# Feature-major layer norms of a hybrid encoder layer: pairwise sums, a running sum, and one more product run ahead

## The chip, the cores and the metric

The kernel runs on one core of a Trainium2 chip. The metric is the device time of one execution in microseconds (us); of several runs the median is given. The matmul engine is called PE, VectorE is DVE, ScalarE is ACT, GpSimd is POOL and SyncE, which issues the DMAs, is SP.

## The reference

One encoder layer is computed for 1024 prompt frames and 64 frames of a running stream, 1088 tokens of 1024 features, all in fp32:

```python
z = x @ w_in                                  # 1024 -> 8200 columns
y_a = silu(layer_norm(dw, ln_a_g, ln_a_b)) @ w_a_out      # dw: causal depthwise conv of a GLU
y_b = (sigmoid(z_o) * hn) @ w_b_out                       # hn: normed mLSTM output
merged = sigmoid(g_a) * y_a + sigmoid(g_b) * y_b
x1 = layer_norm(ALPHA * x + merged @ w_out, ln1_g, ln1_b)
ff = square(relu(x1 @ w_ff1)) @ w_ff2
x2 = layer_norm(ALPHA * x1 + ff, ln2_g, ln2_b)
```

A `layer_norm` takes mean and variance over the 1024 features of a token. The outputs are `x2` and the convolution's and mLSTM's last states. The change touches the first two of the three layer norms, `ln_a` and `ln1`.

## The kernel before, in words

**Layout.** From the input projection to the last feed-forward block, activations are held feature-major: a tile `[128, 8, 384]` has feature `k*128+p` at partition `p`, slot `k`, and tokens along the columns. The 1088 tokens are cut into three chunks of 384, 384 and 320 (`CHUNKS`). Every product is made in about fp32 precision from three matmuls of a rounded high part and a low part (`mm3`, L327 to L332: high by high, high by low, low by high), so each operand is first split: ACT copies the high part, DVE subtracts for the low part (`split`, L334 to L342). One output tile of 128 features by one chunk is a *product* (`product`, L312): 8 slots by 3 matmuls, 24 matmuls into one bank of PSUM.

**The norm over partitions.** Since features lie along partitions and slots, `ln_feature` (L670) sums in two steps: over the eight slots on DVE (`total`, L677: a `tensor_reduce` of four slots, twice), and over partitions with a small matmul of that sum by a matrix of 1/1024 (L690, L691, high and low part). Then each half of four slots is centred by DVE in place (L699) and squared by ACT into a tile `sq` (L701), both squares are reduced (L702, L703), added (L704) and split (L705), and six tiny matmuls give the variance token by token (L711, L714). DVE adds epsilon (L716), POOL raises to the power -0.5 (L717), DVE spreads the result on a diagonal (L719), it is split, and two matmuls by ones give it to all partitions (L725, L726). Last, the eight slots are multiplied by it in four pairs (L729) and `finish` scales and shifts on ACT; in `ln1` it also splits each finished pair into `x1h`, `x1l`, the operand of the feed-forward part (L815 to L818). The split after a sum is called through the helper, so it is recorded at L336 (ACT) and L339 (DVE), on the tiles `sh` and `sl`.

**What sets the order.** A norm is a generator that gives way at each `yield`. It sits in a queue (`BG["misc"]`) and is stepped once by `slot()` (L119), which is called after each product is issued; `waits` gives the number of further slots between its parts. So a norm's small matmuls stand in PE's queue behind a set number of products; the first matmul of each part is pinned there (`pin`). The order of all else on each engine's queue is made by a planner when the program is compiled, from what it takes to be ready, and may differ from the order of the text. Each engine works through its own queue in order.

**The stages around the change.** `ln_a` (L740) norms the convolution's output, read back from DRAM chunk by chunk, while `w_b_out` products run. `out_proj` (L830) makes `merged @ w_out` chunk by chunk: for each of eight feature tiles `j` it loads a tile `sx` of x (from the pool `st` of five buffers), makes the product, evicts it with `ALPHA*x` added into `Y2` (L845), and calls `slot()`. When a chunk is done its `ln1` is queued, so it runs beside the next chunk's products. The last chunk's norm is started by hand at `j == 4` (L847) for its first reduction, and goes on beside the first feed-forward products: `first_units` (L995) makes the first two `w_ff1` pieces' products for chunks 0 and 1 only, then the third piece's product for chunk 0 (L1003), and then the two held products of chunk 2, whose operand the last norm has just made. `unit` (L319) takes the product that was run ahead when it comes to that piece. `post_r` (L880) squares the relu and splits sums and differences of it (`hvh`, `hvl`) for the block products of `w_ff2` that follow.

Of the kernel before, what the change touches and what calls it, by code (L numbers as in the profile page):

```python
# [9 lines left out]
F32 = mybir.dt.float32  # L10
F32R = mybir.dt.float32r
AF = mybir.ActivationFunctionType
ALU = mybir.AluOpType
AX = mybir.AxisListType
# [7 lines left out]
P = 128  # L22
KT = D // P
# [7 lines left out]
CN = 384  # L31
# [13 lines left out]
def bcast(ap, shape):  # L45
    return ap.to_broadcast(shape)
# [3 lines left out]
def hybrid_layer(ctx, tc, x_prompt, x_sample, cache_conv, state_C, state_n, state_m, w_in, b_gate,  # L50
# [4 lines left out]
    V, S, G, TE = nc.vector, nc.scalar, nc.gpsimd, nc.tensor  # L55
    w_in = w_in[0]

    def pool(name, bufs=1, stack=ctx, **kw):
        kw.setdefault("reuse_waits", "tile")
        if kw.get("space") is DRAM:  # L60
# [12 lines left out]
    pools = {"whl": pool("whl", 2, stack=whs, side="right"), "psg": pool("psg", 3, stack=pre, space=PSUM),  # L73
             "psm": pool("psm", 5, stack=pre, space=PSUM)}
    stp = pool("st", 5, stack=pre)
# [11 lines left out]
    def gtile():  # L87
        return pools["psg"].tile([P, 512], F32, tag="m", name="g")
# [13 lines left out]
    BG = {"mlstm": deque(), "conv": deque(), "misc": deque()}  # L102
# [12 lines left out]
    def drain(kind):  # L115
        while step(kind):
            pass

    def slot():  # L119
        busy = step("mlstm")  # L120
        CREDIT["conv"] = min(CREDIT["conv"] + (1.0 if busy else 1.7), 4.0)
        while CREDIT["conv"] >= 1.0 and step("conv"):
            CREDIT["conv"] -= 1.0
        step("misc")
# [182 lines left out]
            V.tensor_copy(cols[:n, b:b + nb], ps[:n, 0:nb].rearrange("p c (h z) -> p c h z", z=32)[:, :, :, 0:4])  # L307


    early, later = [], []  # L310

    def product(hi, lo, ci):  # L312
        n = CHUNKS[ci][1]
        ps = gtile()
        for k in range(KT):
            mm3(ps[:, :n], hi[:, k, :], lo[:, k, :], XO["h"][ci][:, k, :n], XO["l"][ci][:, k, :n], k == 0, k == KT - 1)
        return ps

    def unit(hi, lo, post, chunks=(0, 1, 2)):  # L319
        for ci in chunks:  # L320
            ps = early.pop() if early and ci == 0 else product(hi, lo, ci)
            while later:
                later.pop()()
            post(ci, *CHUNKS[ci], ps)
            slot()
# [8 lines left out]
    def split(hi, lo, src, scale=None, pinned=False):  # L334
        if scale is None:
            a = S.activation(hi, src, AF.Copy)  # L336
            if pinned:
                pin(a)
            V.tensor_tensor(lo, src, hi.bitcast(F32), ALU.subtract)  # L339
        else:  # L340
            S.activation(hi, src, AF.Copy, scale=scale)
            V.scalar_tensor_tensor(lo, src, scale, hi.bitcast(F32), ALU.mult, ALU.subtract)  # L342
# [324 lines left out]
            MB.append(fp.tile([P, KT, CN], F32, tag="f", name="mb"))  # L667
        BG["misc"].append(ln_a())

    def ln_feature(y, n, sc, square, finish, waits):  # L670
        def across(p, k=4):
            return bcast(p[:, None, :n], [P, k, n])

        def tiles():
            return (sc.tile([P, CN], d, tag=t, name=t) for t, d in (("s", F32), ("sh", F32R), ("sl", F32R)))

        def total(out, t, m=CN):  # L677
            V.tensor_reduce(out[:, :n], t[:, :, :n].rearrange("p k t -> p t k"), AX.X, ALU.add)  # L678

        s2 = stp.tile([P, CN], F32, tag="st", name="s2")  # L680
        total(s2, y[:, 0:4])
        yield
        s, sh, sl = tiles()
        total(s, y[:, 4:8])
        V.tensor_tensor(s[:, :n], s[:, :n], s2[:, :n], ALU.add)
        split(sh[:, :n], sl[:, :n], s[:, :n])
        for _ in range(waits[0]):
            yield
        pm = mtile()
        pin(TE.matmul(pm[:, :n], mean1, sh[:, :n], start=True, stop=False))  # L690
        TE.matmul(pm[:, :n], mean1, sl[:, :n], start=False, stop=True)  # L691
        s, sh, sl = tiles()
        s2 = sc.tile([P, CN], F32, tag="s2", name="s2")
        if n < CN:
            G.memset(s[:, n:], 0.0)
        sq = []
        for kh in range(2):
            yh = y[:, 4 * kh:4 * kh + 4, :n]
            V.tensor_tensor(yh, yh, across(pm), ALU.subtract)  # L699
            sq.append(square())  # L700
            S.activation(sq[kh][:, :, :n], yh, AF.Square)  # L701
        total(s, sq[0])  # L702
        total(s2, sq[1])  # L703
        V.tensor_tensor(s[:, :n], s[:, :n], s2[:, :n], ALU.add)  # L704
        split(sh, sl, s)  # L705
        for _ in range(waits[1]):
            yield
        pv = mtile()
        for t in range(3):
            ts = slice(t * P, (t + 1) * P)  # L710
            a = TE.matmul(pv[:, 2 * t:2 * t + 2], sh[:, ts], mean1[:, 0:2], start=True, stop=False)  # L711
            if t == 0:
                pin(a)
            TE.matmul(pv[:, 2 * t:2 * t + 2], sl[:, ts], mean1[:, 0:2], start=False, stop=True)  # L714
        st = small.tile([P, 20], F32, tag="ln", name="ln")
        V.tensor_scalar(st[:, 0:3], pv[:, 0:6:2], EPS, None, ALU.add)  # L716
        G.tensor_tensor(st[:, 3:6], st[:, 0:3], bcast(mhalf, [P, 3]), ALU.pow)  # L717
        s, sh, sl = tiles()
        V.tensor_tensor(s.rearrange("p (t q) -> p t q", q=P), bcast(ident[:, None, :], [P, 3, P]),  # L719
                        bcast(st[:, 3:6, None], [P, 3, P]), ALU.mult)  # L720
        split(sh, sl, s)
        for _ in range(waits[2]):
            yield
        pr = mtile()
        pin(TE.matmul(pr[:, :n], ones, sh[:, :n], start=True, stop=False))  # L725
        TE.matmul(pr[:, :n], ones, sl[:, :n], start=False, stop=True)  # L726
        for k0 in range(0, KT, 2):
            yh = y[:, k0:k0 + 2, :n]
            V.tensor_tensor(yh, yh, across(pr, 2), ALU.mult)  # L729
            for k in range(k0, k0 + 2):  # L730
                finish(k, y[:, k, :n])
        yield
# [73 lines left out]


    X1H, X1L, Y2 = [], [], []
    last_ln = []

    def ln1(ci):
        n = CHUNKS[ci][1]

        def finish(k, z):
            S.activation(z, z, AF.Identity, scale=vecs[:, k, R_G1:R_G1 + 1], bias=vecs[:, k, R_B1:R_B1 + 1])  # L815
            if k % 2:
                ks = slice(k - 1, k + 1)
                split(X1H[ci][:, ks, :n], X1L[ci][:, ks, :n], Y2[ci][:, ks, :n])  # L818
        X1H.append(ph.tile([P, KT, CN], F32R, tag="p", name="x1h"))
        X1L.append(pl.tile([P, KT, CN], F32R, tag="p", name="x1l"))  # L820

        def square():
            return pools["lnq" if ci == 2 else "ln1"].tile([P, 4, CN], F32, tag="sq", name="sq")
        yield from ln_feature(Y2[ci], n, pools["ln1"], square, finish, ((1, 3, 2), (1, 3, 1), (1, 2, 1))[ci])
        if ci == 2:
            lnq.close()
            lns.close()
            pools["hw0"] = pool("hw0", 1, stack=win)

    def out_proj():  # L830
        drain("misc")
        enter(1)
        set_operand(MB)
        MH, ML = XO["h"], XO["l"]
        for ci, (o, n) in enumerate(CHUNKS):
            Y2.append(fp.tile([P, KT, CN], F32, tag="f", name="y2"))
            for j in range(KT):
                s = stp.tile([P, CN], F32, tag="st", name="sx")
                nc.sync.dma_start(s[:, :n], xTD[j * P:(j + 1) * P, o:o + n])
                js = slice(j % 4 * P, j % 4 * P + P)  # L840
                ps = gtile()
                for k in range(KT):
                    mm3(ps[:, :n], WOH[j // 4][:, k, js], WOL[j // 4][:, k, js], MH[ci][:, k, :n], ML[ci][:, k, :n],
                        k == 0, k == KT - 1)
                V.scalar_tensor_tensor(Y2[ci][:, j, :n], s[:, :n], ALPHA, ps[:, :n], ALU.mult, ALU.add)  # L845
                slot()
                if ci == 2 and j == 4:  # L847
                    last_ln.append(ln1(ci))
                    next(last_ln[0])
            if ci < 2:  # L850
                BG["misc"].append(ln1(ci))
        drain("misc")
        BG["misc"].append(last_ln[0])
        step("misc")

    N(out_proj)


# [136 lines left out]
    def first_units(kh, hi, lo):  # L995
        post = post_r(0, kh, True)
        unit(hi, lo, post, (0, 1))
        held.append((hi, lo, post))
        if kh == 1:
            pools["whl"] = pools["whl2"]  # L1000
            third = 2 + next(i for i, p in enumerate(pieces) if p[3] == 1)
            wsplit(third)
            early.append(product(*his[third], 0))  # L1003
            drain("misc")
            for h in held:
                unit(*h, (2,))
            whs.close()
            pools["hw1"] = pool("hw1", 1, stack=win)
# [103 lines left out]
    raws, his = {}, {}  # L1112
# [69 lines left out]
```

## Time and profile before

| | us |
|---|---|
| median of 3 runs (1985.12, 1987.09, 1988.74) | 1987.09 |
| the profiled execution, its own time | 1988.86 |
| the profiled execution, span from first to last instruction | 1986.8 |
| PE busy in the span | 1938.1 |
| DVE busy in the span | 1425.0 |
| ACT busy in the span | 642.8 |

The span is what the trace covers; the profiled execution's own time is 2.1 us longer. Mean granted clock of PE was 0.991 of full speed. Rows of groups read: line, engine, operation, tile written and tiles read, shapes, count, then busy us, mean ns of one, and idle time of the engine before them with what ended it.

### The profile page before, as it was taken

The page shows a single profiled execution, that of the slowest core. Times are in us where ns is not written, and L with a number is a line of the kernel's source. Part 1 is how long each engine was busy: PE and PEld are TensorE (multiplying, and loading weights), DVE is VectorE, ACT ScalarE, POOL GpSimd, SP SyncE. Part 2 cuts the span into 40 slices and gives each one's busy share as a digit, 9 for nine tenths or more (in the row PEclk, how much of TensorE's full clock was granted, in tenths as well). Part 3 has the DMA queues.
Part 4 walks back from the last instruction along what each step waited for, and adds up shares of the span by engine and source line. Part 5 has one row for each costly group of instructions (what it writes and reads, how often), then busy time and mean ns, then how long its engine had stood idle before and what let it go on. Part 6 is the DMA issues. An engine that isn't in the chain of part 4 may idle for free.

```text
span 1986.8 us, 30495 instructions
## 1 busy us (share of the span) xinstructions
PE 1938.1 (98%) x12396; PEld 1914.4 (96%) x12396; DVE 1425.0 (72%) x2717; ACT 642.8 (32%) x1206; POOL 124.9 (6%) x232
## 2 busy tenths in 40 slices
PE   8999999999999999999999998999999999999996
PEld 7999999999999999999999998999999999999995
DVE  3856876787678767878874559867685858677547
ACT  4323322332233223323352214523233232414242
POOL 1112210001000100000000000000000000000005
PEclk9999999999999999999999999999999999999998
DMA  4122312121112211226235210111211111111212
GB/s 140 44 79 58 119 48 57 52 74 52 55 34 66 70 55 43 60 93 205 84 102 158 76 42 14 43 54 33 59 38 54 53 44 54 33 54 43 75 43 80
DMA packets 171744, 131.06 MB, mean 66 GB/s; under 512 B 8271, under 2 KB 166463, under 8 KB 171603
## 3 DMA queue, kind: packets, MB, share of 16 engines
q1 hardware_dynamic: 171603, 129.11, 21.7%
q8 instruction: 97, 1.59, 0.3%
q14 instruction: 44, 0.36, 0.1%
HBM read 104.39 MB, written 24.63 MB: 65 GB/s over the span
## 4 chain that ended last, share of the span: by engine, by line
PE 83%; DVE 9%; issue 3%; ACT 1%; POOL 1%; DMA 1%; SPq 0%; POOLq 0%; ACTq 0%; DVEq 0%
PE g L328 26%; PE g L331 26%; PE g L332 26%; DVE s L678 2%; PE m L328 1%; PE m L332 1%; PE m L331 1%; DVE o L1101 1%; DVE acc L567 1%; DVE ln L650 0%; DVE a L699 0%; DVE y L699 0%; PE m L461 0%; DMA x<-in_x_prompt_dram 0%; PE m L1061 0%
## 5 line engine op out<-in xcount | busy, mean ns | idle before, releaser
L328 PE MATMUL g<-xh,wh 128*128 128x384 f32 (+1 forms) x1920 | 637.7, 332 | 0.0
L331 PE MATMUL g<-xl,wh 128*128 128x384 f32 (+1 forms) x1920 | 632.0, 329 | 0.0
L332 PE MATMUL g<-xh,wl 128*128 128x384 f32 (+1 forms) x1920 | 631.5, 329 | 0.0
L328 PEld LDWEIGHTS g<-xh,wh 128*128 128x128 f32 x1920 | 363.7, 189 | 0.4 <-ACT xh L336 0.2
L331 PEld LDWEIGHTS g<-xl,wh 128*128 128x128 f32 x1920 | 363.5, 189 | 0.3
L332 PEld LDWEIGHTS g<-xh,wl 128*128 128x128 f32 x1920 | 363.1, 189 | 0.1
L567 DVE SCALAR_TENSOR_TENSOR acc<-glu,vecs,acc 128x1118 f32<-128x1118 f32 x240 | 331.6, 1382 | 3.5
L336 ACT ACTIVATE wh<-wr 128x1024 fp32r<-128x1024 f32 (+1 forms) x168 | 166.0, 988 | 445.9 <-PE g L331 355.7
L339 DVE TENSOR_TENSOR wl<-wr,wh 128x1024 fp32r<-128x1024 f32 (+1 forms) x168 | 190.7, 1135 | 113.8 <-ACT wh L336 110.9
L328 PE MATMUL g<-x1h,wh 128*128 128x384 f32 (+1 forms) x768 | 253.4, 331 | 0.0
L331 PE MATMUL g<-x1l,wh 128*128 128x384 f32 (+1 forms) x768 | 253.1, 330 | 0.0
L332 PE MATMUL g<-x1h,wl 128*128 128x384 f32 (+1 forms) x768 | 252.8, 329 | 0.0
L331 PE MATMUL g<-hvl,wh 128*128 128x272 f32 x784 | 223.7, 288 | 0.0
L332 PE MATMUL g<-hvh,wl 128*128 128x272 f32 x784 | 221.9, 288 | 0.0
L328 PE MATMUL g<-hvh,wh 128*128 128x272 f32 x784 | 221.4, 290 | 0.0
L977 DVE TENSOR_TENSOR y<-g,y 128x272 f32<-128x272 f32 (+1 forms) x540 | 157.2, 340 | 26.9 <-PE g L332 25.1
L328 PEld LDWEIGHTS g<-hvh,wh 128*128 128x128 f32 x784 | 146.0, 189 | 1.7 <-DVE y L977 1.3
L331 PEld LDWEIGHTS g<-hvl,wh 128*128 128x128 f32 x784 | 147.5, 188 | 0.0
L332 PEld LDWEIGHTS g<-hvh,wl 128*128 128x128 f32 x784 | 146.5, 188 | 0.0
L331 PEld LDWEIGHTS g<-x1l,wh 128*128 128x128 f32 x768 | 144.9, 189 | 0.1
L332 PEld LDWEIGHTS g<-x1h,wl 128*128 128x128 f32 x768 | 144.9, 189 | 0.0
L328 PEld LDWEIGHTS g<-x1h,wh 128*128 128x128 f32 x768 | 144.6, 188 | 0.1
(272 smaller groups left out, 2423.6 us busy)
## 6 DMA issues: line engine op xcount, KB each, us to landing
wr<-in_w_in_dram SPq DMA_DIRECT2D x64, 512.0 KB
wr<-in_w_ff_dram SPq DMA_DIRECT2D x64, 512.0 KB
x<-in_x_prompt_dram SPq DMA_DIRECT2D x8, 512.0 KB
dwT<-acc SPq DMA_DIRECT2D x8, 512.0 KB
wr<-in_w_b_out_dram SPq DMA_DIRECT2D x8, 512.0 KB
wr<-in_w_a_out_dram SPq DMA_DIRECT2D x8, 512.0 KB
wr<-in_w_out_dram SPq DMA_DIRECT2D x8, 512.0 KB
out_dram<-o SPq DMA_DIRECT2D x16, 256.0 KB
```

What stands on the lines that cost most here:

```text
L328: first = TE.matmul(out, lh, rh, start=start, stop=False, skip_group_check=more)
L331: TE.matmul(out, lh, rl, start=False, stop=False, skip_group_check=more)
L332: TE.matmul(out, ll, rh, start=False, stop=stop, skip_group_check=more)
L336: a = S.activation(hi, src, AF.Copy)
L339: V.tensor_tensor(lo, src, hi.bitcast(F32), ALU.subtract)
L567: V.scalar_tensor_tensor(acc, glu[:, j:j + AC], vecs[:, c, j:j + 1], acc, ALU.mult, ALU.add))
L678: V.tensor_reduce(out[:, :n], t[:, :, :n].rearrange("p k t -> p t k"), AX.X, ALU.add)
L977: V.tensor_tensor(y, ps[:, pslc], y, ALU.add)
L1101: V.tensor_tensor(o[:n, hs], o[:n, hs], pools["g2"][:n, hs], ALU.mult)
```

## The change

- Sums over slots are made by pairs: `fold` adds slots 0,1 to slots 2,3 in place (768 elements a partition) and then slot 0 to slot 1 (384). For a first sum over eight slots the halves are added first into a `sq` tile (1536 elements). Each squared half is folded right behind its square; before, both reductions came after both squares.
- `ln1` gets its first sum ready-made: in `out_proj` a tile `YS` from the pool `st` takes up each evicted tile from `j == 1` on, one add behind each eviction. The first sum in `ln_a` is made in one step and split one slot later.
- Slots between parts: `ln1` of chunk 0 has (2, 3, 2) for (1, 3, 2), chunk 1 (2, 3, 2) for (1, 3, 1), chunk 2 (1, 2, 1) as before. The last product of the last chunk calls no slot; the second chunk's norm is then drained, so its last part (L725 on) stands behind that product, and the last chunk's norm is queued and stepped there.
- `early` is a dictionary by chunk. The third piece's products for chunks 0 and 1 are run ahead of the last chunk's products, for chunk 0 alone before.

```diff
-    early, later = [], []
+    early, later = {}, []
...
-            ps = early.pop() if early and ci == 0 else product(hi, lo, ci)
+            ps = early.pop(ci) if ci in early else product(hi, lo, ci)
...
-    def ln_feature(y, n, sc, square, finish, waits):
+    def ln_feature(y, n, sc, square, finish, waits, total=None):
...
-        def total(out, t, m=CN):
-            V.tensor_reduce(out[:, :n], t[:, :, :n].rearrange("p k t -> p t k"), AX.X, ALU.add)
-
-        s2 = stp.tile([P, CN], F32, tag="st", name="s2")
-        total(s2, y[:, 0:4])
-        yield
+        def fold(out, t):
+            V.tensor_tensor(t[:, 0:2, :n], t[:, 0:2, :n], t[:, 2:4, :n], ALU.add)
+            V.tensor_tensor(out[:, :n], t[:, 0, :n], t[:, 1, :n], ALU.add)
+
         s, sh, sl = tiles()
-        total(s, y[:, 4:8])
-        V.tensor_tensor(s[:, :n], s[:, :n], s2[:, :n], ALU.add)
-        split(sh[:, :n], sl[:, :n], s[:, :n])
+        if total is None:
+            t = square()
+            V.tensor_tensor(t[:, :, :n], y[:, 0:4, :n], y[:, 4:8, :n], ALU.add)
+            fold(s, t)
+            total = s
+            yield
+        split(sh[:, :n], sl[:, :n], total[:, :n])
...
-        sq = []
-        for kh in range(2):
+        for kh, part in enumerate((s, s2)):
             yh = y[:, 4 * kh:4 * kh + 4, :n]
             V.tensor_tensor(yh, yh, across(pm), ALU.subtract)
-            sq.append(square())
-            S.activation(sq[kh][:, :, :n], yh, AF.Square)
-        total(s, sq[0])
-        total(s2, sq[1])
+            sq = square()
+            S.activation(sq[:, :, :n], yh, AF.Square)
+            fold(part, sq)
...
-        yield from ln_feature(Y2[ci], n, pools["ln1"], square, finish, ((1, 3, 2), (1, 3, 1), (1, 2, 1))[ci])
+        yield from ln_feature(Y2[ci], n, pools["ln1"], square, finish, ((2, 3, 2), (2, 3, 2), (1, 2, 1))[ci], YS[ci])
...
-                slot()
-                if ci == 2 and j == 4:
-                    last_ln.append(ln1(ci))
-                    next(last_ln[0])
-            if ci < 2:
-                BG["misc"].append(ln1(ci))
-        drain("misc")
-        BG["misc"].append(last_ln[0])
+                if j == 1:
+                    YS.append(stp.tile([P, CN], F32, tag="st", name="ys"))
+                if j:
+                    V.tensor_tensor(YS[ci][:, :n], Y2[ci][:, 0, :n] if j == 1 else YS[ci][:, :n], Y2[ci][:, j, :n], ALU.add)
+                if ci < 2 or j < KT - 1:
+                    slot()
+            if ci == 2:
+                drain("misc")
+            BG["misc"].append(ln1(ci))
         step("misc")
...
-            early.append(product(*his[third], 0))
+            for ci in range(2):
+                early[ci] = product(*his[third], ci)
```

More of the change, by code (lines that the diff above doesn't have):

```diff
@@ L808, in hybrid_layer @@
     X1H, X1L, Y2 = [], [], []
-    last_ln = []
+    YS = []
     def ln1(ci):
```

## The prediction

> **What bounds the kernel now.** I read the page's shares first, then the waits of the matmul engine (PE), then the table of time windows around those waits, then groups by form and the timelines of VectorE (DVE) and ScalarE (ACT) inside them.
>
> ```profile
> span 1986.8 us, 30495 instructions
> PE 1938.1 (98%) x12396; PEld 1914.4 (96%) x12396; DVE 1425.0 (72%) x2717; ACT 642.8 (32%) x1206; POOL 124.9 (6%) x232
> ```
>
> PE is busy for 98% of the span. No work of PE is removed by this change, so all it can win is PE's waits and what follows each of them. Where they lie:
>
> ```profile
> PE m L445 <- DVE isb L523: 7.0, 3, 2.5
> ...
> PE m L714 <- DVE sl L339: 4.8, 3, 2.3
> PE m L711 <- ACT sh L336: 4.7, 2, 2.9
> PE m L690 <- ACT sh L336: 2.6, 2, 1.9
> PE m L725 <- ACT sh L336: 2.0, 2, 1.6
> ...
> PE m L726 <- DVE sl L339: 0.5, 1, 0.5
> ...
> PE m L691 <- DVE sl L339: 0.3, 1, 0.3
> ```
>
> Columns: total us, times, longest. L690 to L726 are the small matmuls of `ln_feature`: together 4.8+4.7+2.6+2.0+0.5+0.3 = 14.9 us. The first row lies elsewhere and stays. Behind the norms nothing else is late:
>
> ```profile
> 1130.00:1260.00 130.00, 120.08 (x695) 118.18 (x694) 87.25 (x92) 40.60 (x59) 3.55 (x4) 0.96 0.11 32
> 1260.00:1960.00 700.00, 699.22 (x4729) 689.16 (x4728) 494.42 (x1261) 226.88 (x436) 18.14 (x30) 1.00 0.16 49
> ```
>
> After the stretch, PE's and the window's times, come PE's busy time, weight loads, DVE, ACT, POOL, clock, DMA share and GB/s. PE lacks 9.9 us where `ln1` runs and 0.8 us in the 700 us behind it. So a microsecond won before 1260 reaches the end.
>
> A wait costs more than its idle time:
>
> ```profile
> 1140.00:1160.00 20.00, 20.00 (x115) 20.00 (x115) 6.91 (x9) 0.53 (x1) 0.00 (x0) 1.00 0.20 56
> 1202.00:1211.00 9.00, 9.00 (x63) 9.00 (x63) 8.97 (x6) 2.98 (x2) 0.00 (x0) 1.00 0.13 38
> 980.50:987.50 7.00, 4.87 (x22) 4.72 (x21) 6.03 (x7) 0.71 (x2) 0.86 (x1) 0.76 0.36 109
> 1174.80:1188.10 13.30, 11.00 (x57) 10.87 (x56) 4.87 (x7) 0.52 (x2) 0.85 (x1) 0.87 0.09 26
> 1211.30:1220.00 8.70, 5.78 (x30) 5.51 (x29) 4.85 (x8) 1.04 (x2) 0.85 (x1) 0.80 0.00 1
> 1239.10:1247.80 8.70, 6.93 (x34) 6.61 (x33) 5.98 (x10) 1.43 (x3) 1.70 (x1) 0.80 0.37 119
> ```
>
> Undisturbed, a 384-column matmul takes 20/115 = 0.174 us and a 320-column one 9/62 = 0.145 (63 touch that window, one only in part). The fourth window holds 48 of the former (8.4 us) and six tiny ones (some 0.7 with edges): 9.1 of its 13.3, so 4.2 lost, of which 2.3 idle. Likewise lost: 3.6 (980), 4.5 (1211), 3.5 (1239). The granted clock of 0.76 to 0.87 is the rest. The Trainium skill ("TensorE: Matmul & The Clock Gate", Part 1) puts the half clock behind an idle window of about 3.4 us; by that alone only the idle 14.9 us would be at stake, but here idle stretches of 1.8 to 2.9 us show it, so the rows decide. The shorter waits I price at idle plus 0.5. In `ln1`: L690 once 2.6−1.9 = 0.7, so 1.2, and once 1.9 with L691's 0.3, so 2.7. In `ln_a`: L714's third, 0.4, bare; L725 once 2.0−1.6 = 0.4 with L726's 0.5, so 1.5 (first chunk), and once 1.6, so 2.1 (third). All norms lose 0.4+1.5+3.6+2.1+4.2+1.2+4.5+2.7+3.5 = 23.7 us.
>
> **The folds instead of reductions.**
>
> ```profile
> L678 DVE TENSOR_REDUCE s<-y 128x384 f32<-128x1536 f32 x4 | 11.6, 2906 | 0.1
> L678 DVE TENSOR_REDUCE s<-sq 128x384 f32<-128x1536 f32 x4 | 11.6, 2898 | 1.1 <-ACT sq L701 1.1
> L339 DVE TENSOR_TENSOR x1l<-y,x1h 128x768 fp32r<-128x768 f32 x8 | 7.6, 956 | 0.3
> L699 DVE TENSOR_TENSOR y<-y,m 128x1536 f32<-128x1536 f32 x4 | 6.8, 1750 | 0.1
> L678 DVE TENSOR_REDUCE s<-sq 128x320 f32<-128x1280 f32 x2 | 4.8, 2459 | 0.0
> L685 DVE TENSOR_TENSOR s<-s,s 128x384 f32<-128x384 f32 x2 | 1.1, 558 | 0.0
> ```
>
> A fold is one add of 768 elements and one of 384: 0.96+0.56 = 1.52 us for a reduction's 2.90; at 320 columns by proportion 1.3 for 2.46. Each squared half saves 1.4 (1.15), twice per chunk. An `ln_a` first sum becomes 1.75+1.52 = 3.3 for 2×2.9+0.56 = 6.4. An `ln1` first sum leaves the chain: 7 adds of 0.56, each behind its product's eviction, while PE takes 4.2 us for a product. The Trainium skill ("VectorE: DVE Perf Modes", the perf-mode table) gives `tensor_reduce` one element a cycle, as for an fp32 `tensor_tensor`; by that a reduction would last like L699, 1.75 us, and a fold would win only 0.2. The reduction's row, 2.90, says otherwise.
>
> **`ln1` beside the second and third chunk of the output product.**
>
> ```profile
> 1165.84 2.93 DVE L678 TENSOR_REDUCE s<-sq 128x384 f32<-128x1536 f32 x1
> 1168.67 0.56 DVE L845 SCALAR_TENSOR_TENSOR y<-sx,g 128x384 f32<-128x384 f32 x1
> 1170.32 2.93 DVE L678 TENSOR_REDUCE s<-sq 128x384 f32<-128x1536 f32 x1 [1.10 <-ACT sq L701]
> ...
> 1173.63 0.55 DVE L704 TENSOR_TENSOR s<-s,s 128x384 f32<-128x384 f32 x1
> 1174.10 2.80 DVE L678 TENSOR_REDUCE s<-y 128x384 f32<-128x1536 f32 x1
> 1176.82 0.55 DVE L339 TENSOR_TENSOR sl<-s,sh 128x384 fp32r<-128x384 f32 x1
> ```
>
> PE had come to L711 at 1174.8. The squares' sums ended at 1173.2, and then a first sum of the *next* chunk stood before `sl`. That last reduction goes; the chain from the second subtraction's end (1165.9) becomes fold 1.5, second square 1.5 (one `sq` buffer, so it waits for the fold), an eviction and its running add 1.1, fold 1.5, add and split 1.6: 7.2, so 1173.1, 1.7 before PE. **4.2 gained.** In the third chunk PE needs 72×0.145 = 10.5 us from L691 to L711. The chain there is two subtractions 3.4, fold, square, fold 4.5, add and split 1.6, and 0.5 to 1.5 of evictions and adds: 10.0 to 11.0. L690's first wait goes, because its sum is ready one product earlier. I take 0.3 as left: **1.2+4.5−0.3 = 5.4** (3 to 5.7).
>
> The extra cost of the running sums is 21 adds, 0.5 us each, with DVE at 87 of 130 us here; cover gone, each would delay a bank's return by 0.5, and there are three banks. The sum sits in one of the five `st` buffers that also take the `sx` loads (rival three). The first chunk's extra slot before its mean costs nothing: it stands in for the reduction's slot.
>
> **`ln_a`.**
>
> ```profile
> 950.05 2.89 DVE L678 TENSOR_REDUCE s<-a 128x384 f32<-128x1536 f32 x1
> ...
> 954.87 1.22 DVE L339 TENSOR_TENSOR wl<-wr,wh 128x1024 fp32r<-128x1024 f32 x1
> ...
> 1013.09 3.55 DVE L339 TENSOR_TENSOR xl<-a,xh 128x768 fp32r<-128x768 f32 x4
> ```
>
> The 980 wait (3.6) goes: two folds leave DVE 2.8 us earlier against 7.0−4.9 = 2.1 idle. So does the 0.4. The first chunk's 1.5 (L725, L726) stands behind the reduction at 950, placed ahead of the small steps, and a weight split; a 1.75 us add can take the reduction's place, so I count 0.5. The third chunk's 2.1 stands behind the splits of the next operand (1013), which stay. The first add now waits for both loaded halves, with the `mb` evictions behind it on DVE; since PE never waited at the first L690 with 6.4 us of sum before it, 3.3 us started one load later has 3 to spare, and I count nothing. **4.5** (2 to 6.5).
>
> **The seam to the feed-forward part.** The second chunk's scaling (L725, L729, `finish`) moves from before the last output product to behind it, with its 4 splits. What bounds it:
>
> ```profile
> L815 ACT ACTIVATE y<-y,vecs 128x384 f32<-128x384 f32 x16 | 10.4, 696 | 12.0 <-DVE y L729 12.0
> L336 ACT ACTIVATE x1h<-y 128x768 fp32r<-128x768 f32 x8 | 6.7, 832 | 0.0
> ...
> 1223.87 0.34 PE L328 MATMUL g<-x1h,wh 128*128 128x384 f32 x1
> ...
> 1230.76 0.41 PE L691 MATMUL m<-sl,mean 128*128 128x320 f32 x1 [0.30 <-DVE sl L339]
> ...
> 1241.27 0.27 PE L711 MATMUL m<-mean,sh 128*128 128x2 f32 x1 [1.77 <-ACT sh L336]
> ```
>
> Count from the last output product's end (1223.9). Before, L711 came 17.4 later where matmuls need 24×0.174+0.35+48×0.174 = 12.9; with the clock the stretch lost 2.7+3.5 = 6.2. After: scaling starts at 0.5; a quarter costs ACT 2×0.70+0.83 = 2.2, so four end near 11 and their low parts near 11.5. PE would want the last quarter at 0.35+4.2+0.35+3×1.04 = 8.0: up to 3.5 of new wait, unless the second piece's product over the ready first chunk is planned into it. The mean's `sl` queues behind multiplications and one split, near 5.8. From L691 (6.3) the old chain took 10; folds save 2.3, two later splits of 0.96 now fall into it: 9.6, L711 at 15.9 against PE's 13.2. Lost 2.7 idle and 1.7 of clock, 4.4 for 6.2: **1.8 gained** (−5 to 6).
>
> **The product run ahead.** It is moved, not added, and issues no DMA (nor does the moved scaling; no queue of SP or POOL is passed): 24×0.174 = 4.2 us of cover for the last chunk's splits. No wait at that chunk's products stands among PE's waits above, so it is worth 0 unless ACT lags. It has a price: the held products finish 4 us later while what follows stays, so the operand splits for the block products crowd.
>
> ```profile
> 1260.00:1280.00 20.00, 20.00 (x126) 20.00 (x125) 18.44 (x37) 12.63 (x26) 0.00 (x0) 1.00 0.09 27
> ```
>
> DVE has 1.6 us to spare in these 20; 4.2 us less leaves 2.6 late, less what slack the operands have. I take **−1.5** (−4 to 0). Beside it, one PSUM bank more is held, of eight.
>
> **Sum:** 4.5+4.2+5.4+1.8−1.5 = 14.4 us. The profiled execution took 1988.9 (span 1986.8), so it would take 1974.5; the median shown, 1987.1, is 1.8 lower and gives 1972.7.
>
> **Rivals.**
> One: the seam eats the gain. The pinned L690 and the late quarters wait in turn, 12 us lost for 6.2, and the block products wait 4. Then 14.1−6−4 = 4 to 8 us gained, 1981. For it: scaling now starts a product later; against: ready products can be planned into the gap. Chance 0.18.
> Two: the planner that orders each queue puts other long steps before `sl` (as it put the reduction at 1174), and waits of equal price return: 0 to 3 us, 1986. For it: L726 at 956 waited behind the 1.2 us weight split at 954.87, which stays. Against: nothing left in `ln1`'s chain is over 1.75. Chance 0.05.
> Three, slower: `YS` leaves four `st` buffers for the loads, so each must land within three products, 10.5 to 12.5 us.
>
> ```profile
> 3.53 8.51 DMA x<-in_x_prompt_dram
> ...
> sx<-xTD SPq DMA_DIRECT2D x16, 192.0 KB
> ```
>
> A load of 512 KB took 8.5 us, so 192 KB should land in time. At 16 us each of 24 products would take 16/3 = 5.3 instead of 4.0: 31 lost, 2003; it outweighs the 14 from about 14 us on. Chance 0.03.
>
> **How the numbers follow.** The forecast has 0.74. A measurement of this kernel can tell 0.2% (4 us) from no change. Faster by more: 0.74 and nearly all of rival one, 0.91; within: 0.06; slower: 0.03. The terms' bounds added in full would give 0 to 24; together the terms seldom all miss one way, so I take 21 to 7 gained: 1966 to 1980, which holds the forecast and some of rival one.
>
> **What would show it.** Right: no L678, DVE some 30 us less busy (24 reductions out, folds and adds in), no wait at L714 over 0.5 near 983 and 1177, none at L711 near 1214, the window 1130 to 1260 lacking about 4 us for 9.9. The seam is right if L711 still waits 1 to 3 us; wrong if the second chunk's first feed-forward product waits more than 4. A new wait on `hv` operands at the first block product would show the crowding; waits on `sx` at L845, rival three. No gain at all would refute that PE's waits at the norms carry to the end.

## The result, and the profile after

The changed kernel takes 1972.05 us, median of four runs (1971.82 to 1975.75), beside 1987.91 of the kernel before on the same chip: a ratio of 0.9925, with an interval of 0.9910 to 0.9941. The forecast was 1972.7, in a range of 1966 to 1980. The total was hit; two of its five terms were not, and they offset each other, which is luck. One execution of e7 and one of e8 took 3161 and 3164 us at a mean granted clock of 0.557, and the medians below are of the others.

The page's shares, after:

```profile
span 1970.0 us, 30522 instructions
PE 1932.2 (98%) x12396; PEld 1909.1 (97%) x12396; DVE 1393.5 (71%) x2741; ACT 642.6 (33%) x1206; POOL 124.7 (6%) x232
```

The span is 16.8 us shorter, PE has the same 12396 matmuls, and DVE is 31.5 us less busy. PE's waits by releaser, after (total us, times, longest):

```profile
PE g L331 <- DVE x1l L339: 1.5, 2, 1.0
PE m L711 <- ACT sh L336: 1.4, 1, 1.4
PE m L693 <- DVE sl L339: 1.0, 1, 1.0
...
PE g L328 <- DVE y L976: 0.5, 2, 0.3
```

L693 is what L691 was. Of the 14.9 us at the small matmuls of the norms 2.4 are left, and all of it stands at one place, the seam between the output product and the feed-forward part. Two waits are new: L331 on `x1l`, at the seam too, and L328 on a block product's eviction. The groups that took the reductions' place, DVE from the output product to the first block product:

```profile
L849 DVE TENSOR_TENSOR ys<-ys,y 128x384 f32<-128x384 f32 x12 | 6.7, 554 | 0.2
L678 DVE TENSOR_TENSOR sq<-sq 128x768 f32<-128x768 f32 x4 | 3.8, 952 | 1.1 <-ACT sq L702 1.1
...
L679 DVE TENSOR_TENSOR s<-sq 128x384 f32<-128x384 f32 x4 | 2.2, 549 | 0.0
```

A fold takes 0.95+0.55 = 1.50 us, as the rows of before had it (1.52).

Where the time went is read best by four marks on PE's timeline: the first mean of `ln_a`, the first output product, the first feed-forward product, the first block product. Of before (the third mark is in the prediction):

```profile
937.42 0.34 PE L690 MATMUL m<-sh,mean 128*128 128x384 f32 x1
...
1115.36 0.34 PE L328 MATMUL g<-xh,woh 128*128 128x384 f32 x1
...
1279.20 0.29 PE L328 MATMUL g<-hvh,wh 128*128 128x272 f32 x1
```

and of after:

```profile
935.03 0.34 PE L692 MATMUL m<-sh,mean 128*128 128x384 f32 x1
...
1105.22 0.34 PE L328 MATMUL g<-xh,woh 128*128 128x384 f32 x1
...
1203.94 0.34 PE L328 MATMUL g<-x1h,wh 128*128 128x384 f32 x1
...
1261.84 0.29 PE L328 MATMUL g<-hvh,wh 128*128 128x272 f32 x1
```

The first mark is 2.4 us earlier, though PE's instructions up to it are the same, in the same order. That is chance: a second trace of the changed kernel has it at 938.5. So stages between marks say more of the change than spans do. All kernels below by their own marks, in us. The experiments ran on different chips, but the median of the kernel before was 1987.5 to 1987.9 beside each of the medians shown, so these can be read side by side.

| kernel | first mean to output product | output product to feed-forward | seam: to first block product | first to last block product | median, us |
|---|---|---|---|---|---|
| before | 177.9 | 108.5 | 55.3 | 584.3 | 1987.91 |
| changed | 170.2 | 98.7 | 57.9 | 585.4 | 1972.05 |
| changed, second trace (e0) | 170.2 | 98.7 | 56.3 | 585.4 | 1974.54 |
| one product ahead (e1) | 170.2 | 98.7 | 58.1 | 584.3 | 1972.75 |
| early scaling (e2) | 170.2 | 99.0 | 52.5 | 585.4 | 1969.51 |
| squares folded alone (e3) | 171.2 | 101.2 | 54.3 | 584.3 | 1973.00 |
| all but the squares' folds (e4) | 174.6 | 101.7 | 60.6 | 585.4 | 1983.56 |
| early scaling, variance later (e5) | 170.2 | 99.0 | 50.7 | 586.2 | 1968.35 |
| early scaling, one ahead (e6) | 170.2 | 99.0 | 52.8 | 584.3 | 1967.14 |
| neighbours' reductions (e7) | 170.0 | 99.2 | 51.7 | 584.4 | 1965.97 |
| adds in place (e8, stages of e10) | 170.2 | 98.5 | 52.9 | 584.2 | 1968.17 |

The change won 7.7 us beside `ln_a`, 9.8 in the output product, and gave back 1.0 to 2.6 at the seam and 1.1 in the block products. Of the signs that the prediction had set, its window of 130 us lacks 4.1 us of PE, for about 4 forecast and 9.9 before (it stands at 1114 to 1244 now), and DVE never waits for a load of `sx` at L845: rival three's cost did not come.

### The profile page after: what moved, and what is told of

Same layout as the page of the kernel before. It is cut to its first block, busy times and chain, and to the rows that moved or that the text cites. A ratio compares the mean times of both kernels' runs of the same rounds, so it can differ in the third digit from the quotient of the medians.

```text
span 1970.0 us, 30522 instructions
## 1 busy us (share of the span) xinstructions
PE 1932.2 (98%) x12396; PEld 1909.1 (97%) x12396; DVE 1393.5 (71%) x2741; ACT 642.6 (33%) x1206; POOL 124.7 (6%) x232
## 4 chain that ended last, share of the span: by engine, by line
PE 89%; DVE 6%; issue 2%; POOL 1%; ACT 1%; DMA 1%; SPq 0%; POOLq 0%; ACTq 0%
PE g L328 27%; PE g L331 27%; PE g L332 27%; PE m L328 1%; PE m L332 1%; PE m L331 1%; DVE o L1103 1%; DVE acc L567 1%; DVE ln L650 1%; PE m L461 0%; DMA x<-in_x_prompt_dram 0%; PE m L408 0%; PE m L1063 0%; PE m L467 0%; PE m L168 0%
## 5 line engine op out<-in xcount | busy, mean ns | idle before, releaser
L328 PE MATMUL g<-xh,wh 128*128 128x384 f32 (+1 forms) x1920 | 635.4, 331 | 0.0
L331 PE MATMUL g<-xl,wh 128*128 128x384 f32 (+1 forms) x1920 | 629.9, 328 | 0.0
L328 PEld LDWEIGHTS g<-xh,wh 128*128 128x128 f32 x1920 | 361.9, 189 | 0.3
L331 PEld LDWEIGHTS g<-xl,wh 128*128 128x128 f32 x1920 | 361.9, 188 | 0.2
L331 PE MATMUL g<-x1l,wh 128*128 128x384 f32 (+1 forms) x768 | 254.0, 331 | 1.5 <-DVE x1l L339 1.5
L328 PE MATMUL g<-x1h,wh 128*128 128x384 f32 (+1 forms) x768 | 254.3, 331 | 0.1
L331 PE MATMUL g<-hvl,wh 128*128 128x272 f32 x784 | 223.4, 287 | 0.0
L328 PE MATMUL g<-hvh,wh 128*128 128x272 f32 x784 | 221.2, 290 | 0.5 <-DVE y L976 0.5
L328 PEld LDWEIGHTS g<-hvh,wh 128*128 128x128 f32 x784 | 145.8, 189 | 2.6 <-DVE y L978 1.4
L331 PEld LDWEIGHTS g<-x1l,wh 128*128 128x128 f32 x768 | 145.2, 189 | 2.4 <-DVE x1l L339 2.4
L331 PEld LDWEIGHTS g<-hvl,wh 128*128 128x128 f32 x784 | 147.3, 188 | 0.0
L328 PEld LDWEIGHTS g<-x1h,wh 128*128 128x128 f32 x768 | 145.2, 189 | 0.6 <-ACT x1h L336 0.5
```

What stands on the lines that cost most here:

```text
L328: first = TE.matmul(out, lh, rh, start=start, stop=False, skip_group_check=more)
L331: TE.matmul(out, lh, rl, start=False, stop=False, skip_group_check=more)
```

## The experiments

The theory: what PE waited for at the norms was the length of the steps that stand on DVE between a norm's small ones, so the folds carry the gain; and the seam loses because the second chunk's scaling went behind the last output product. The rivals were that the queue's order or the first sum's place on the chain decides, and that DVE and ACT are short of time at the seam wherever the scaling stands.

**e3, the squares' folds alone**, put into the kernel before:

```diff
...
-        sq = []
-        for kh in range(2):
+        for kh, part in enumerate((s, s2)):
...
-            sq.append(square())
-            S.activation(sq[kh][:, :, :n], yh, AF.Square)
-        total(s, sq[0])
-        total(s2, sq[1])
+            sq = square()
+            S.activation(sq[:, :, :n], yh, AF.Square)
+            fold(part, sq)
```

> The kernel before with folds for the sums of squares alone; all first sums by reductions, slots and products run ahead as before. Theory (each wait is the length of DVE's chain): the waits at L711 (2.9 and 1.8) and L714 at 983 go or fall under 1 us since 2.8 us leave each chain; the wait at L714 near 1177, made by a first-sum reduction placed ahead of sl, and the one at L690 near 1230 stay in part. 8 to 11 us won: 1977 to 1980. Rival (the queue's order decides, not the length): the first-sum reductions are placed ahead of sl again and the waits stay; 0 to 4 us won, 1984 to 1988.

Measured: 1973.00 us (0.9935, 0.9921 to 0.9948), 4 us below what the theory gave, and not told apart from the whole change. PE's waits from 900 to 1300 us of it:

```profile
PE m L694 <- ACT sh L336: 2.6, 2, 1.8
PE m L713 <- ACT sh L336: 1.6, 2, 1.0
PE m L716 <- DVE sl L339: 0.5, 2, 0.3
```

L694, L713 and L716 are the mean and the variance. The wait for the mean (2.6) is what it was: its sum is still made by reductions. The variance's waits fell from 4.7+4.8 to 1.6+0.5, and with them the slow clock behind them: in the four stretches behind the variance it is 1.00, where it was 0.76 to 0.87, and only behind the mean's 1.8 us is it still low, at 0.79. The wait near 1177 fell to 0.2 too, which the theory had left standing in part. This is the place that decides against the queue's order as the cause: the planner put a first-sum reduction of 2.94 us ahead of `sl` again (at 1163.40, for the one at 1174.10 before), and still the wait is 0.2 us for 2.3, because the squares' sums end sooner.

**e4, all of the change but the squares' folds**:

```diff
             sq = square()
             S.activation(sq[:, :, :n], yh, AF.Square)
-            fold(part, sq)
+            V.tensor_reduce(part[:, :n], sq[:, :, :n].rearrange("p k t -> p t k"), AX.X, ALU.add)
```

> The changed kernel with the sums of squares by reductions again, one behind each square; running sums, folded first sums of ln_a, slots and products ahead as changed. Theory (length of the chain): each chain from the mean to L711 is 2.8 us longer, so L711 waits 1 to 3 us in the third chunk of the output product and 3 to 5 at the seam, with the clock behind each; 5 to 9 us lost against the changed kernel: 1977 to 1981. Rival (what was in the way was the first sums' reductions): without them the squares' sums fit, 0 to 3 us lost, 1972 to 1975.

Measured: 1983.56 us (0.9981, 0.9972 to 0.9989), 11.5 above the change, more than either side gave. Its largest waits, 900 to 1300 us:

```profile
PE m L711 <- ACT sh L336: 4.8, 3, 2.6
PE m L725 <- ACT sh L336: 1.6, 1, 1.6
PE g L331 <- DVE x1l L339: 1.5, 2, 1.0
PE m L714 <- DVE sl L339: 1.4, 3, 0.7
...
```

The variance waits are back, at 4.8+1.4 for 4.7+4.8. So the running sum, the folded first sums, the moved slots and the second product ahead together win 4 us by themselves; the squares' folds win 15 by themselves. By stages the 4 us are 3.3 and 6.8 won beside the norms and 5.3 lost at the seam, where the scaling stands late here too. Beside the norms the two parts would add up to 24.1, and the change won 17.5 there: a wait that one of them ends leaves nothing for the other.

**e2, the scaling early**:

```diff
-        yield from ln_feature(Y2[ci], n, pools["ln1"], square, finish, ((2, 3, 2), (2, 3, 2), (1, 2, 1))[ci], YS[ci])
+        yield from ln_feature(Y2[ci], n, pools["ln1"], square, finish, ((2, 3, 2), (2, 3, 1), (1, 2, 1))[ci], YS[ci])
```

> The changed kernel with the second chunk's last part (L725 on) one product earlier, ahead of the last output product, as in the kernel before: waits (2, 3, 1) for (2, 3, 2). Theory: the seam's loss (2.7 us of idle at L693, L331 and L328, 5.7 with the clock, then 3.3 around L711) comes from the scaling being behind the last product; now x1l is ready when its product comes, the first loss falls under 1.5, sl is no longer behind the scaling, L711's wait stays within 1 us of what it was, and the time is 1967 to 1969. Rival: ACT and DVE are short of time at the seam wherever the scaling stands; then the wait only moves to L711, which waits 3 to 5 us, and the time stays within 1 us of 1972.

Measured: 1969.51 us (0.9912, 0.9899 to 0.9926). The median is half a microsecond above the theory's 1967 to 1969 and 2.5 below the change; the two intervals overlap, so the traces must decide. By the marks the seam fell from 57.9 (56.3 in the second trace) to 52.5, with 0.3 lost before it. In the changed kernel PE stood at the seam for these, by its timeline:

```profile
1209.46 0.41 PE L693 MATMUL m<-sl,mean 128*128 128x320 f32 x1 [1.04 <-DVE sl L339]
...
1213.09 0.44 PE L331 MATMUL g<-x1l,wh 128*128 128x384 f32 x1 [0.55 <-DVE x1l L339]
...
1215.77 0.69 PE L331 MATMUL g<-x1l,wh 128*128 128x384 f32 x1 [0.96 <-DVE x1l L339]
...
1224.05 0.27 PE L711 MATMUL m<-mean,sh 128*128 128x2 f32 x1 [1.41 <-ACT sh L336]
```

and with the scaling early for these:

```profile
1211.34 0.41 PE L692 MATMUL m<-sh,mean 128*128 128x320 f32 x1 [1.00 <-ACT sh L336]
...
1222.36 0.27 PE L711 MATMUL m<-mean,sh 128*128 128x2 f32 x1 [1.75 <-ACT sh L336]
```

No wait on `x1l` is left, and L711 waits 1.75 us, not 3 to 5. The rival falls: the place of the scaling made the seam's loss. Idle time is the smaller part of it: PE idled 4.1 us in the seam of the changed kernel and 2.9 here, and the rest of the 5.4 us is matmuls that ran longer, at a mean granted clock of 0.94 for 1.00 here.

**e1, one product ahead**:

```diff
-            for ci in range(2):
-                early[ci] = product(*his[third], ci)
+            early[0] = product(*his[third], 0)
```

> The changed kernel with one product run ahead (chunk 0) in place of two. Theory: the second one covers nothing, because four quarters of the last chunk's operand come 2 us apart and two held products can share each quarter; it only moves work and crowds DVE before the first block product. Then no wait appears at the held products, the waits of L328 on L976 (0.5 us, some 1.0 with the clock) go, and the time is 1971 (0 to 1.5 us less than the changed kernel's 1972). Rival: PE comes sooner to the held products than in the kernel before, waits there for x1l, and the time is 1974 to 1976.

Measured: 1972.75 us (0.9931, 0.9918 to 0.9943), 1.75 above what the theory gave, and not told apart from the change by its median. By the marks the block products fell from 585.4 to 584.3 and the seam from 57.9 went to 58.1, with no wait at the held products, and none at L976. The rival's wait does not appear: the second product ahead covers nothing here and costs the first block products 1.1 us.

**e6, early scaling and one product ahead**, both edits together:

> The changed kernel with the second chunk's scaling ahead of the last output product and one product run ahead in place of two: the folds and the running sum with the slots' places of the kernel before. Theory: the seam is 52.5 us as with two ahead, the waits on L976 at the first block product go (1.0 us): 1967.5 to 1969.5, 3 to 5 us under the kernel before with folds for the squares alone (1973.0), which is what the running sum and the folded first sums are worth by themselves. Rival: PE, without the waits before, reaches the held products before their operand; the seam takes 54 to 56 us, 1970 to 1972, and the second product ahead is needed after all.

Measured: 1967.14 us (0.9896, 0.9882 to 0.9909), 0.4 below the theory's band; stages 99.0, 52.8 and 584.3, so the rival's seam of 54 to 56 did not come. Run once more as e9, below, 1968.08. This version is faster than both kernels; beside it on the same chip the changed kernel itself (e0) took 1974.54 (0.9931, 0.9919 to 0.9944).

> The changed kernel itself once more, beside the three others. Both theories: 1970 to 1974 us; from the first feed-forward product to the first block product 57.9 us as in its first trace, whatever the parts before the norms take by chance.

The median lies half a microsecond over what was expected, and its seam took 56.3 in place of 57.9; the last section comes back to that.

**e5, the last chunk's variance one product later**, on top of the early scaling, with two products ahead:

```diff
-        yield from ln_feature(Y2[ci], n, pools["ln1"], square, finish, ((2, 3, 2), (2, 3, 2), (1, 2, 1))[ci], YS[ci])
+        yield from ln_feature(Y2[ci], n, pools["ln1"], square, finish, ((2, 3, 2), (2, 3, 1), (1, 3, 1))[ci], YS[ci])
...
-            for ci in range(2):
-                early[ci] = product(*his[third], ci)
+            early[0] = product(*his[third], 0)
+            slot()
+            early[1] = product(*his[third], 1)
```

> The changed kernel with the second chunk's scaling ahead of the last output product (waits (2, 3, 1)) and the last chunk's variance one product later (waits (1, 3, 1), one more slot between the two products run ahead). Theory: what was left at the seam is L711's wait (1.75 us, 2.1 with the clock), because PE reaches it after two products and the chain from the mean needs 10 us; behind three products it is gone, and the second product run ahead now covers the scaling. The seam from the first feed-forward product to the first block product takes 50 to 51 us (52.5 with the early scaling alone, 57.9 in the changed kernel), the time is 1966 to 1968. Rival: the later scaling leaves the held products without their operand; they wait as much as was won, and the seam stays at 52 to 54 us, 1968 to 1971.

Measured: 1968.35 us (0.9903, 0.9888 to 0.9918), 0.35 over the theory's band and in the rival's, its seam 50.7, as the theory had it. L711's wait is gone, and none stands at the held products:

```profile
PE g L328 <- DVE y L976: 1.3, 2, 1.0
PE m L692 <- ACT sh L336: 1.0, 1, 1.0
```

but the first block products now wait 1.3 us for DVE, and their stage grew to 586.2. Of the 2.1 us that the seam is shorter than in e6, 1.9 are paid there.

**e7, reductions over neighbours**, in the kernel before:

```diff
-            V.tensor_reduce(out[:, :n], t[:, :, :n].rearrange("p k t -> p t k"), AX.X, ALU.add)
+            V.tensor_reduce(out[:, :n].rearrange("p (k t) -> p k t", k=4), t[:, :, :n].rearrange("p k (t g) -> p k t g", g=4), AX.X, ALU.add)
```

> The kernel before, in which each reduction sums four neighbouring tokens of a slot in place of the four slots of a token: as many elements in and out, but read one behind the other (the norms' statistics are then of other elements). Theory (the stride of 384 elements is what makes a reduction slow): each takes 1.6 to 1.9 us for 2.9, as the Trainium skill's rule of one element a cycle has it; the chains are 2 us shorter, most waits go as with the folds, and the time is 1974 to 1980. Rival (the reduction itself is slow): each takes 2.8 to 3.0, and the time stays 1986 to 1989.

Measured: 1965.97 us (0.9892, 0.9877 to 0.9907), 8 below the lower end that the theory gave. Its outputs are not the layer's: it leaves out the sum over slots. The reductions:

```profile
L678 DVE TENSOR_REDUCE s<-y 128x384 f32<-128x1536 f32 x4 | 7.0, 1750 | 0.1
L678 DVE TENSOR_REDUCE s<-sq 128x384 f32<-128x1536 f32 x4 | 7.0, 1746 | 1.1 <-ACT sq L701 1.1
```

The same instruction on as many elements takes 1.75 us where they lie one behind the other, and 2.90 at a stride of 384 elements. The kernel's structure is that of before, without running sum, moved slots or second product; beside the second chunk of the output product DVE takes the norm's steps in the order of before, the first-sum reduction ahead of `sl` among them; and it is as fast as e6. That leaves the length of the steps.

**e8, adds in place.** That result left it open whether the running sum is needed at all. Here each half of a first sum is three adds of 384 elements at its old place, and the squares are folded as in e3:

```diff
-            V.tensor_reduce(out[:, :n], t[:, :, :n].rearrange("p k t -> p t k"), AX.X, ALU.add)
+            V.tensor_tensor(out[:, :n], t[:, 0, :n], t[:, 1, :n], ALU.add)
+            for k in (2, 3):
+                V.tensor_tensor(out[:, :n], out[:, :n], t[:, k, :n], ALU.add)
...
```

> The kernel before with every reduction replaced by adds where it stood: the squares folded, each half of a first sum by three adds of 384 elements (3 x 0.56 = 1.7 us for 2.9). No running sum, slots and products ahead as before. Theory (all that matters is how long the steps are that stand between a norm's small ones on DVE): it takes what the kernel with neighbours' reductions took, 1965 to 1969 us, and the running sum, the moved scaling and the second product ahead are not needed for it. Rival (the first sum has to leave the chain): it stays near the folds of the squares alone, 1971 to 1974, 4 to 7 us behind the running sum with the early scaling.

> The changed kernel with the early scaling and one product ahead once more, beside the one above: 1966 to 1969 us; its stage from the first output product to the first feed-forward product 99 us, the seam 52.8. By the theory within 2 us of the kernel above, by the rival 4 to 7 us ahead of it.

Measured on one chip: e8 1968.17 us (0.9900, 0.9884 to 0.9917), e9 1968.08 (0.9902, 0.9887 to 0.9917). They can't be told apart. A further execution of e8's kernel gives its stages:

> The kernel with adds in place once more, for a profile at the full clock: 1965 to 1969 us. By the theory its stages are 170 us from the first mean to the first output product, 99 to the first feed-forward product and 51 to 53 from there to the first block product (neighbours' reductions: 170.0, 99.2, 51.7). By the rival the output product's stage takes 101 or more, as with the squares alone.

It took 1966.83 us; its stages are 170.2, 98.5 and 52.9, beside 170.2, 99.0 and 52.8 of e6. The rival falls: the first sum may stay on the chain if its steps are short.

## Why the prediction was right, point by point, and where not

**PE's waits at the norms carry to the end**, and a wait is worth more than its idle time: right. 14.9 us of idle were at stake, 12.5 went, and the two stages up to the seam became 17.5 us shorter, where 14.1 had been forecast.

**A fold takes 1.52 us for 2.90**: right (1.50). The Trainium skill's rule of one element a cycle ("VectorE: DVE Perf Modes", the perf-mode table) was set aside for the reduction because the row said 2.90. The row was what mattered for this change, but in e7 a reduction of elements that lie side by side took 1.75 us, as L699's step on as many elements did; that agrees with the rule, and the stride makes the difference. Read so, the rule would have shown a second way to the same gain.

**The output product, 4.2+5.4 = 9.6**: right; 108.5−98.7 = 9.8. The chain from the second subtraction's end to `sl` took 7.6 us in the second chunk, for 7.2 as worked, and the trace has no wait of PE at either norm of that stage.

**`ln_a`, 4.5 (2 to 6.5)**: too small, and outside its own bounds; 7.7 measured. The step that failed: "The third chunk's 2.1 stands behind the splits of the next operand (1013), which stay." The splits stayed, the wait went. DVE's timeline, after:

```profile
1002.88 3.56 DVE L339 TENSOR_TENSOR xl<-a,xh 128x768 fp32r<-128x768 f32 x4 [0.18 <-ACT xh L336]
...
1006.83 0.15 DVE L716 TENSOR_SCALAR ln<-m 128x3 f32<-128x3 f32 x1
```

PE came to L711 at 1005.64. The sums end sooner, so the four splits begin 2.8 us ahead of L711; before they began 1.0 ahead of it (1013.09 for 1014.04) and kept DVE from L716 until 1017.02. They are over when L716 is due. Shorter sums of squares are what it takes: with folds for them alone (e3) the wait is gone, without (e4) L725 waits 1.6 again. The first chunk's 1.5 at L725 and L726 went whole, where 0.5 had been counted. With both, the prediction's own prices give 3.6+0.4+1.5+2.1 = 7.6.

**The seam, +1.8 (−5 to 6)**: wrong in sign, within its bounds; 55.3 became 57.9 and, in the second trace, 56.3. The step that failed: "two later splits of 0.96 now fall into it: 9.6", the chain from the mean to the variance. The mean came when it was worked to come (L693 5.5 us behind the last output product, for 6.3), but L711 came 14.6 us behind it. What stood on DVE between the two, up to the first centring:

```profile
1210.14 0.96 DVE L339 TENSOR_TENSOR x1l<-y,x1h 128x768 fp32r<-128x768 f32 x1 [0.73 <-ACT x1h L336]
1212.08 0.96 DVE L339 TENSOR_TENSOR x1l<-y,x1h 128x768 fp32r<-128x768 f32 x1 [0.98 <-ACT x1h L336]
1213.62 1.23 DVE L339 TENSOR_TENSOR wl<-wr,wh 128x1024 fp32r<-128x1024 f32 x1 [0.58 <-ACT wh L336]
1214.76 0.95 DVE L339 TENSOR_TENSOR x1l<-y,x1h 128x768 fp32r<-128x768 f32 x1
1215.63 1.48 DVE L700 TENSOR_TENSOR y<-y,m 128x1280 f32<-128x1280 f32 x1
```

These are not two splits but three and a weight split, and DVE waited 2.3 us among them for ACT to make their high parts. The prediction had the last low part near 11.5 us, and it ended at 11.8; but the centring stood behind it, and by the sum it would have stood ahead. So the loss, "2.7 idle and 1.7 of clock, 4.4 for 6.2", was mis-sized. The waits are of the kinds described: `sl` behind multiplications and a split (L693, 1.04), the late quarters (0.55 and 0.96), for which the sum held nothing, and the variance (1.41). Before, 6.2 of 55.3 us were lost by the prediction's count; by the same count 8.8 of 57.9 are lost now, 7.2 in the second trace. The four waits are 4.0 us of this, and the rest, 4.8 or 3.2, is matmuls that ran longer. Three of the four waits stand in these 12 us:

```profile
1208.00:1220.00 12.00, 9.27 (x38) 7.69 (x37) 9.70 (x12) 10.28 (x15) 0.00 (x0) 0.86 0.13 45
```

The trace has 38 matmuls here, where 69 would run at 0.174 each, and the granted clock was 0.86. The sign that was to show the seam right, a wait of 1 to 3 us at L711, came (1.41) and could not tell this loss from a gain. e2 shows that the move of the scaling is the cause. This is rival one's mechanism, at a fifth to two fifths of its price: 1.0 to 2.6 at the seam and 1.1 in the block products, for 5.8 and 4.

**The second product ahead, 0 for cover and −1.5 for crowding**: right; −1.1 by e1 and e6, and e5 shows the same crowding grow. The new wait stands at a block product's eviction (L976), not at the `hv` operands that were to show it.

**The sum** was 14.4. By stages it is 7.7+9.8−2.6−1.1 = 13.8, and with the second trace's seam 15.4. What `ln_a` gave beyond its term, 3.2, the seam took: 4.4 or 2.8. The medians differ by 15.9; measured again beside the kernel before (e0), by 13.2. That the median came within 0.7 us of the forecast is luck, in the terms and in the measurement.

**What bought it.** The prediction spread the gain over folds and running sum by where each wait stood. The runs put it otherwise: folds for the squares alone won 15 us (e3), all the sums' steps made short in their old places won 19 (e8) and 22 (e7), and the running sum adds nothing that could be measured to adds in place (e8, e9).

## What to carry to other kernels

Where a matmul engine waits a few microseconds at each of several small steps, first look for the one long instruction that stands in the small steps' queue, and ask whether its access pattern makes it long; a cheaper form of it in the old place may win all that a new structure would. Gains from two cures of one chain don't add, so test each alone. When late work is moved behind a product to shorten one wait, work out what its results' readers do meanwhile: the seam lost here what the edit was to gain, and putting the scaling back, with one product ahead, gave 5 to 7 us more.

## What the runs showed of the hardware that was not expected

The price of a wait varies from one execution to the next. The changed kernel waits 1.41 us at L711 in both of its traces. The windows of 8.3 us around it, in the first trace and in the second:

```profile
1222.30:1230.60 8.30, 6.89 (x33) 6.58 (x33) 3.34 (x8) 1.54 (x3) 0.85 (x1) 0.79 0.18 63
```

```profile
1225.70:1234.00 8.30, 6.89 (x43) 6.58 (x42) 4.46 (x10) 2.23 (x5) 0.85 (x1) 1.00 0.19 63
```

The same stretch, the same idle time, and 33 matmuls at a clock of 0.79 or 43 at 1.00. That is the 1.6 us between the two seams. The other runs show the same of waits of this size: behind 1.75 us at the variance of the last chunk the clock was 1.00 in e2 and in e10, behind 1.77 us in the kernel before 0.80. Each single wait of over 2 us at the norms lowered it: 2.13, 2.30 and 2.92 us in the kernel before (0.76, 0.87 and 0.80 over the prediction's windows) and 2.56 us in e4 (0.66). The Trainium skill ("TensorE: Matmul & The Clock Gate", Part 1) has the activity window run freely beside the program, which agrees with one wait having two prices; that it takes an idle window of 3.4 us to lower the clock does not, since no wait at the norms was as long as that. Waits like this may be a part of what makes runs of one kernel differ by some microseconds; that was not tried.
